# RMSNorm and matmul on one core: eight token tiles per transfer, gamma read first, two short reads halfway

## The chip, the core and the metric

The kernel runs on one core of a Trainium2 chip. Time is the device time of one execution in microseconds (us); the figure used is the median of ten runs. The profile is of one further execution.

A core has five engines that run side by side and wait for each other through semaphores. TensorE (PE) multiplies matrices, and its weight loads are shown as PEld. VectorE (DVE), ScalarE (ACT) and GpSimd (POOL) work on tiles. SyncE (SP) issues most of the transfers. The transfers between HBM and the core's memory run on 16 DMA engines, which every queue shares.

## What is computed

```python
# x: 16 x 1024 x 512 float32, gamma: 512 ones, weight: 512 x 768 float32, eps: 1e-5
rms = np.sqrt(np.mean(x ** 2, axis=-1, keepdims=True) + eps)
x_norm = x / rms * gamma
return np.matmul(x_norm, weight).astype(np.float32)
```

The output is 16 x 1024 x 768 float32. The kernel reads 33.6 MB of x and 1.6 MB of weights and writes 50.3 MB.

## The kernel before

**Tiling.** The 16,384 rows of x are 128 token tiles of 128 rows. A tile of x is 256 KB, a tile of the output 384 KB. The kernel works on pairs of tiles (`j`, 64 of them). Gamma is multiplied into the weights once (`weights`), so that a tile needs only its own row scale at the end.

**Work of one tile.** GpSimd casts x to bf16 (L85, a pair at a time). TensorE transposes the cast tile, taken as 32-bit words of two bf16 values (L112, two transposes a tile). VectorE copies the transposed words out of the accumulator memory (L119). ScalarE squares and sums the rows (L89) and takes the root (L93), VectorE the reciprocal (L95). TensorE then runs eight matmuls a tile, four of 512 and four of 256 columns (L146). The result is scaled by the reciprocal and written to an output tile: even tiles on ScalarE (L129), odd tiles on VectorE (L131). The transposes of later tiles are put between the matmuls (`feeder`).

**Transfers.** Consecutive tiles are grouped, `G = 4` to a group. `parts` says into how many transfers a group is cut: the first three and the last three groups are cut smaller, and all others are moved whole. In `rows` a transfer of t tiles gives each of the 128 partitions t rows that follow each other in HBM. A load of four tiles thus has 128 pieces of 8 KB, and a store of four tiles 128 pieces of 12 KB. Loads go into eight buffers of four tiles (`xin`), results into four buffers of four tiles (`out`). A group's store is issued when its last tile is scaled (L143).

**Order.** The order on each engine is written out by hand (`manual_schedule`); a loop iteration issues the load of the group four ahead, then the work of a pair. All loads and nearly all stores are issued by SP, in the order of the program, so a load that stands behind a store is issued after it. The last two tiles have four stores of their own, two on ScalarE's queue and two on SP's (L291). SP's and ScalarE's transfers take turns on eight completion semaphores: a transfer is issued only when the earlier one with the same semaphore has landed.

**Start.** The first tiles of x are loaded ahead of the weights, and gamma is read between them by ScalarE (L184). TensorE runs 14 matmuls on zeros (`warm_up`, L204) around the first transposes, and the transpose of gamma (L214) stands after the first three of them. The first three tiles are multiplied with the first half of the weights as soon as that is scaled.

Of the kernel before, what the change touches and what calls it, by code (L numbers as in the profile page):

```python
# [12 lines left out]
F32 = mybir.dt.float32  # L13
# [5 lines left out]
def kernel(  # L19
# [8 lines left out]
    nc = tc.nc  # L28
    P = 128

    x = x.flatten_outer_dims()
    out = out.flatten_outer_dims()
    N, D = x.shape
    _, O = out.shape
    K = D // P
    NT = N // P
    NP = NT // 2
    G = 4
    NG = NT // G
    PF = 5  # L40
    WIDE = 512

    parts = {0: [1, 2, 1], 1: [2, 2], 2: [2, 2], NG - 3: [2, 2], NG - 2: [2, 2], NG - 1: [1, 1, 1, 1]}
    first, size = {}, {}
    for g in range(NG):
        i = g * G
        for n in parts.get(g, [G]):
            for t in range(n):  # L50
# [3 lines left out]
    def rows(ap, i):  # L54
        return ap[first[i] * P:(first[i] + size[i]) * P, :].rearrange("(p t) d -> p t d", t=size[i])

    singles = ctx.enter_context(tc.tile_pool(name="singles", bufs=1))
    xin = ctx.enter_context(tc.tile_pool(name="xin", bufs=PF + 3))
    xbp = ctx.enter_context(tc.tile_pool(name="xb", bufs=4))
    junk = ctx.enter_context(tc.tile_pool(name="junk", bufs=2))  # L60
    stats = ctx.enter_context(tc.tile_pool(name="stats", bufs=4))
    xt_pool = ctx.enter_context(tc.tile_pool(name="xt", bufs=4))
    tpsum = ctx.enter_context(tc.tile_pool(name="tpsum", bufs=2, space=bass.MemoryType.PSUM))
    opsum = ctx.enter_context(tc.tile_pool(name="opsum", bufs=3, space=bass.MemoryType.PSUM))
    outp = ctx.enter_context(tc.tile_pool(name="out", bufs=4))

    x_tiles, xb_tiles, tp_tiles, rstd_of, xT_tiles, o_tiles = {}, {}, {}, {}, {}, {}

    def held(tiles, i, n=1):
        return tiles[i // G][:, i % G:i % G + n, :]  # L70

    def load(i):
        if i // G not in x_tiles:
            x_tiles[i // G] = xin.tile([P, G, D], F32, name="xt")
        nc.sync.dma_start(out=held(x_tiles, i, size[i]), in_=rows(x, i))

    def load_group(g):
        for i in range(g * G, (g + 1) * G):
            if first[i] == i:
                load(i)  # L80

    def cast(i, engine, n=1):
        if i // 2 not in xb_tiles:
            xb_tiles[i // 2] = xbp.tile([P, 2, D], BF16, name="xb")
        engine.tensor_copy(out=xb_tiles[i // 2][:, i % 2:i % 2 + n, :], in_=held(x_tiles, i, n))  # L85

    def square(i, ssq):
        jk = junk.tile([P, D], BF16, name="jk")
        nc.scalar.activation(out=jk, in_=held(x_tiles, i)[:, 0, :], func=AF.Square, accum_out=ssq)  # L89

    def root(i, n, ssq):
        rms = stats.tile([P, 4], F32, name="rms")
        nc.scalar.activation(out=rms[:, :n], in_=ssq[:, :n], func=AF.Sqrt, scale=1.0 / D, bias=eps_sb)  # L93
        rstd = stats.tile([P, 4], F32, name="rstd")
        nc.vector.reciprocal(out=rstd[:, :n], in_=rms[:, :n])  # L95
        for t in range(n):
            rstd_of[i + t] = rstd[:, t:t + 1]
# [24 lines left out]
    def transpose_tile(i):  # L122
        for h in range(2):
            transpose_word(i // 2, i % 2, h)
        evac(i // 2, i % 2, 1)

    def scale(engine, dst, src, r):
        if engine is nc.scalar:
            nc.scalar.mul(out=dst, in_=src, mul=r)  # L129
        else:  # L130
            nc.vector.tensor_single_scalar(out=dst, in_=src, scalar=r, op=mybir.AluOpType.mult)  # L131

    def accumulator():
        return opsum.tile([P, 2, WIDE], F32, name="ops").rearrange("p a b -> p (a b)")
# [15 lines left out]
    def matmuls(i, acc, ks, feed=None):  # L150
        for k in ks:
            matmul(i, k, acc, 0, WIDE)
            if feed:
                feed()
            matmul(i, k, acc, WIDE, O)
# [18 lines left out]
        return feed  # L174

    with tc.manual_schedule():

        wv = weight.rearrange("(h w c) o -> w h (c o)", w=P, c=2)
        touched = singles.tile([P, 2, 1], F32)
        nc.scalar.dma_start(out=touched, in_=wv[:, :, 0:1])  # L180
        load(0)
        load(1)
        g_row = singles.tile([2, P, 2], F32)
        nc.scalar.dma_start(out=g_row, in_=gamma.rearrange("(h w c) -> h w c", w=P, c=2))  # L184
        nc.scalar.preload_act_table(AF.Sqrt)  # L185
        w_f32 = singles.tile([P, K, O], F32)
        for h in range(2):
            nc.sync.dma_start(out=w_f32[:, 2 * h:2 * h + 2, :].rearrange("p c o -> p (c o)"), in_=wv[:, h, :])
        load(3)
        for g in range(1, PF):  # L190
            load_group(g)


        warm = singles.tile([P, WIDE], BF16)
        nc.vector.memset(warm, 0.0)  # L195
        eps_sb = singles.tile([P, 1], F32)
        nc.vector.memset(eps_sb, float(eps))  # L197
        ident_f = singles.tile([P, P], F32)
        make_identity(nc, ident_f)
        spare = accumulator()  # L200

        def warm_up(n):
            for _ in range(n):
                nc.tensor.matmul(out=spare[:, :WIDE], lhsT=warm[:, :P], rhs=warm, start=True, stop=True)  # L204

        w_bf = singles.tile([P, K, O], BF16)

        def weights(k, engine):
            scale(engine, w_bf[:, k, :], w_f32[:, k, :], g_sb[:, k % 2, k // 2:k // 2 + 1])

        warm_up(3)
        gp = tpsum.tile([P, 2, 2], F32, name="tp")
        for c in range(2):
            nc.tensor.transpose(out=gp[:, c, :], in_=g_row[:, :, c], identity=ident_f[:2, :2])  # L214
        g_sb = singles.tile([P, 2, 2], F32)
        nc.vector.tensor_copy(out=g_sb, in_=gp)  # L216
        warm_up(3)


        ssq = stats.tile([P, 4], F32, name="ssq")  # L220
        cast(0, nc.vector)
        square(0, ssq[:, 0:1])
        transpose_tile(0)
        warm_up(3)
        cast(1, nc.vector)
        cast(2, nc.gpsimd)
        square(1, ssq[:, 1:2])
        square(2, ssq[:, 2:3])
        transpose_tile(1)
        transpose_tile(2)  # L230
        warm_up(5)

        acc = [accumulator() for _ in range(4)]
        weights(0, nc.vector)
        weights(1, nc.scalar)
        for k in (0, 1):
            for i in range(3):
                matmuls(i, acc[i], [k])
        root(0, 3, ssq)
        weights(2, nc.vector)  # L240
        weights(3, nc.scalar)
        cast(3, nc.gpsimd)
        matmuls(0, acc[0], [2, 3])
        finish_tile(0, acc[0], nc.scalar)
        transpose_tile(3)
        norms(3, 1)
        matmuls(1, acc[1], [2, 3])
        finish_tile(1, acc[1], nc.vector)
        cast(4, nc.gpsimd)
        cast(5, nc.gpsimd)  # L250
        matmuls(2, acc[2], [2, 3])
        finish_tile(2, acc[2], nc.scalar)
        matmuls(3, acc[3], [0, 1, 2, 3], feeder([2], [0, 2, 2, 0], alone=True))
        finish_tile(3, acc[3], nc.vector)
        cast(6, nc.gpsimd, 2)
        cast(8, nc.gpsimd, 2)
        norms(4, 2)


        one, two, both = [1, 1, 0, 1, 1, 0, 0, 0], [1, 0, 1, 0, 1, 0, 1, 0], [1, 1, 1, 1, 1, 1, 1, 1]  # L260
        for j in range(2, NP):
            if j % 2 == 0 and j // 2 + PF - 1 < NG:
                load_group(j // 2 + PF - 1)
            if j + 3 < NP:
                cast(2 * j + 6, nc.gpsimd, 2)
            if j + 1 < NP:
                norms(2 * j + 2, 2)
            if j == NP - 1:
                break
            if j < 4:  # L270
                feed = feeder([j + 1], one)
            elif j == 4:
                feed = feeder([5, 6], both)
            elif j + 2 < NP:
                feed = feeder([j + 2], two)
            else:
                feed = None
            for i, engine in ((2 * j, nc.scalar), (2 * j + 1, nc.vector)):
                a = accumulator()
                matmuls(i, a, range(K), feed)  # L280
                finish_tile(i, a, engine)


        for i in (NT - 2, NT - 1):
            for lo, hi, engine, queue in ((0, WIDE, nc.scalar, nc.scalar), (WIDE, O, nc.vector, nc.sync)):
                a = accumulator()
                for k in range(K):
                    matmul(i, k, a, lo, hi)
                dst = out_tile(i)[:, lo:hi]
                scale(engine, dst, a[:, lo:hi], rstd_of[i])  # L290
                queue.dma_start(out=rows(out, i)[:, 0, lo:hi], in_=dst)  # L291
# [35 lines left out]
```

## Time and profile before

| what | value |
|---|---|
| median of 10 runs | 213.34 us (213.13 to 214.67) |
| the profiled execution's own time | 213.34 us |
| its span, first to last instruction | 211.6 us |
| TensorE busy | 200.6 us, 95% of the span |
| ScalarE busy | 158.1 us, 75% |
| VectorE busy | 111.3 us, 53% |
| GpSimd busy | 65.1 us, 31% |
| bytes moved | 85.70 MB, mean 405 GB/s |
| packets | 12,678 |

The span is what the page calls the time from the first to the last instruction. The run's own time is 1.7 us longer than that. The page divides the span into 40 slices of 5.3 us and gives the busy share of each engine in tenths for every slice, the mean busy share of the 16 DMA engines, and the rate at which they moved bytes. Another part of the page follows the chain of work that ended last back through the execution. Lists of groups give each kind of instruction with its count, its mean duration and what ended the idle time ahead of it.

### The profile page before, as it was taken

To read this page: it belongs to the slowest core of one execution; us is meant where nothing else is said; L and a number is where in the kernel's file an instruction comes from. 1 tells how busy PE (TensorE), PEld (TensorE's weight loads), DVE (VectorE), ACT (ScalarE), POOL (GpSimd) and SP (SyncE) were. 2 spreads that over 40 slices of the span, in tenths; PEclk is the share of its full clock that TensorE was granted. 3 is DMA by queue.
4 is the path that set the end of the run, shared out by engine and by line. 5 is a ranking of instruction groups with operands and counts; after the bars stand their busy time and mean duration, and the time that the engine had idled before them with its cause. 6 is when DMAs were issued, how large, how long until landed. Compare 5 with 4: busy or idle time off the path is not lost.

```text
span 211.6 us, 3631 instructions
## 1 busy us (share of the span) xinstructions
PE 200.6 (95%) x1271; PEld 138.5 (65%) x1296; DVE 111.3 (53%) x203; ACT 158.1 (75%) x388; POOL 65.1 (31%) x71
## 2 busy tenths in 40 slices
PE   5999999999999999999999999999999999999960
PEld 2566767766776677777667776776777777667630
DVE  1536556545654565456545654664466446545630
ACT  4469877877787778777877887788778877877830
POOL 2075332133332233333223333322233333223000
PEclk9999999999999999999999999999999999999996
DMA  6999999999999999999999999999999999999892
GB/s 233 410 419 369 419 421 423 395 429 412 428 424 420 422 417 428 424 426 421 430 428 417 420 426 425 428 424 424 431 422 429 428 423 419 417 420 414 342 385 112
DMA packets 12678, 85.70 MB, mean 405 GB/s; under 512 B 1650, under 2 KB 1908, under 8 KB 6004
## 3 DMA queue, kind: packets, MB, share of 16 engines
q1 hardware_dynamic: 12096, 84.94, 96.9%
q10 hardware_dynamic: 564, 0.53, 0.7%
q8 instruction: 10, 0.16, 0.3%
q14 instruction: 8, 0.07, 0.1%
HBM read 35.13 MB, written 50.33 MB: 404 GB/s over the span
## 4 chain that ended last, share of the span: by engine, by line
PE 93%; DMA 1%; DVE 1%; ACT 1%; issue 1%; ACTq 0%
PE ops L146 77%; PE tp L112 13%; PE ops L204 2%; DMA g_row<-in_gamma_dram 1%; DVE ot L131 1%; ACT ot L129 0%; ACT jk L89 0%; ACTq L180 0%; DVE xT L119 0%; PE tp L214 0%; ACT rms L93 0%; DVE rstd L95 0%
## 5 line engine op out<-in xcount | busy, mean ns | idle before, releaser
L146 PE MATMUL ops<-w_bf,xT 128*128 128x512 bf16 (+1 forms) x999 | 192.5, 324 | 1.3
L146 PEld LDWEIGHTS <-xT 128*128 128x128 bf16 x1024 | 100.3, 98 | 56.5 <-DVE xT L119 0.9
L85 POOL CAST xb<-xt 128x1024 bf16<-128x1024 f32 (+1 forms) x65 | 64.5, 1014 | 126.9 <-DMA xt<-in_x_dram 92.3
L119 DVE COPY xT<-tp 128x1024 bf16<-128x1024 bf16 (+1 forms) x67 | 44.6, 667 | 83.2 <-PE tp L112 83.1
L129 ACT ACTIVATE ot<-ops,rstd 128x768 f32<-128x768 f32 (+1 forms) x65 | 58.1, 894 | 38.9 <-PE ops L146 38.1
L89 ACT ACTIVATE jk<-xt 128x512 bf16<-128x512 f32 x128 | 78.8, 618 | 0.9 <-DMA xt<-in_x_dram 0.9
L112 PE MATMUL tp<-ident_f,xb 128*128 128x128 f32 x256 | 69.4, 276 | 0.1
L131 DVE TENSOR_SCALAR ot<-ops,rstd 128x768 f32<-128x768 f32 (+1 forms) x65 | 64.5, 992 | 2.9 <-PE ops L146 2.8
L112 PEld LDWEIGHTS tp<-ident_f,xb 128*128 128x128 f32 x256 | 36.4, 143 | 4.0 <-issue 0.7
L89 ACT ACTIVATION_READ_ACCUMULATOR jk<-xt 128x1 f32 x128 | 24.3, 190 | 0.0
L93 ACT ACTIVATE rms<-ssq,eps_sb 128x2 f32<-128x2 f32 (+1 forms) x64 | 18.9, 295 | 2.0
L95 DVE RECIPROCAL rstd<-rms 128x2 f32<-128x2 f32 (+1 forms) x64 | 9.9, 155 | 3.1 <-ACT rms L93 3.1
L204 PE MATMUL ops<-warm 128*128 128x512 bf16 x14 | 6.7, 624 | 1.2 <-DVE eps_sb L197 1.2
L129 ACT ACTIVATE w_bf<-w_f,g_sb 128x768 bf16<-128x768 f32 x2 | 1.9, 936 | 2.8 <-DVE xT L119 2.2
L204 PEld LDWEIGHTS <-warm 128*128 128x128 bf16 x14 | 1.8, 139 | 3.0 <-issue 1.7
L185 ACT ACT_TABLE_LOAD x1 | 1.3, 1283 | 1.9 <-issue 1.9
L216 DVE COPY g_sb<-tp 128x4 f32<-128x4 f32 x1 | 0.2, 163 | 3.1 <-PE tp L214 3.1
L214 PEld LDWEIGHTS tp<-ident_f,g_row 2*128 2x128 f32 x2 | 0.3, 201 | 2.1 <-issue 2.1
L214 PE MATMUL tp<-ident_f,g_row 2*128 2x2 f32 x2 | 0.4, 250 | 1.2 <-DMA g_row<-in_gamma_dram 1.2
L131 DVE TENSOR_SCALAR w_bf<-w_f,g_sb 128x768 bf16<-128x768 f32 x2 | 1.2, 614 | 0.5 <-DMA w_f<-in_weight_dram 0.5
L85 DVE CAST xb<-xt 128x512 bf16<-128x512 f32 x2 | 0.8, 416 | 0.0
L195 DVE MEMSET warm<- 128x256 uint32 x1 | 0.3, 272 | 0.9 <-PEq L308 0.9
(7 smaller groups left out, 1.0 us busy)
## 6 DMA issues: line engine op xcount, KB each, us to landing
out_dram<-ot SPq DMA_DIRECT2D x26, 1536.0 KB, 10.9
xt<-in_x_dram SPq DMA_DIRECT2D x26, 1024.0 KB, 12.7
out_dram<-ot SPq DMA_DIRECT2D x9, 768.0 KB, 9.3
xt<-in_x_dram SPq DMA_DIRECT2D x9, 512.0 KB, 10.5
xt<-in_x_dram SPq DMA_DIRECT2D x6, 256.0 KB, 12.5
w_f<-in_weight_dram SPq DMA_DIRECT2D x2, 768.0 KB, 7.3
out_dram<-ot SPq DMA_DIRECT2D x4, 384.0 KB, 7.7
out_dram<-ot ACTq DMA_DIRECT2D x2, 256.0 KB, 5.5
```

The source lines that it names most:

```text
L85: engine.tensor_copy(out=xb_tiles[i // 2][:, i % 2:i % 2 + n, :], in_=held(x_tiles, i, n))
L89: nc.scalar.activation(out=jk, in_=held(x_tiles, i)[:, 0, :], func=AF.Square, accum_out=ssq)
L93: nc.scalar.activation(out=rms[:, :n], in_=ssq[:, :n], func=AF.Sqrt, scale=1.0 / D, bias=eps_sb)
L95: nc.vector.reciprocal(out=rstd[:, :n], in_=rms[:, :n])
L112: nc.tensor.transpose(out=tp_tiles[j][:, t, h, :], in_=words[:, lo:lo + P], identity=ident_f)
L119: nc.vector.tensor_copy(out=dst[:, t:t + n, :], in_=src[:, t:t + n, :])
L129: nc.scalar.mul(out=dst, in_=src, mul=r)
L131: nc.vector.tensor_single_scalar(out=dst, in_=src, scalar=r, op=mybir.AluOpType.mult)
L146: nc.tensor.matmul(out=acc[:, lo:hi], lhsT=xT_tiles[i // 2][:, i % 2, k // 2, :, k % 2], rhs=w_bf[:, k, lo:hi], start=(k == 0), stop=(k == ...
L185: nc.scalar.preload_act_table(AF.Sqrt)
L204: nc.tensor.matmul(out=spare[:, :WIDE], lhsT=warm[:, :P], rhs=warm, start=True, stop=True)
L214: nc.tensor.transpose(out=gp[:, c, :], in_=g_row[:, :, c], identity=ident_f[:2, :2])
```

## The change

Groups become eight tiles instead of four. The first two groups and the last two are cut smaller. In the middle, from tile 16 to tile 111, each load and each store is one transfer of eight tiles, with 16 KB and 24 KB per partition. There are five input buffers of eight tiles and three output buffers of eight tiles. Loads are started by tile number (`load_until`) instead of by group. Gamma's read is the first on ScalarE's queue. Its transpose and copy move behind the transposes of tiles 0 to 2, the zero matmuls are arranged as 6, 3 and 6 instead of 3, 3, 3 and 5, and the scaling of the first quarter of the weights is cut in two. At pair 32 two reads of 5 and 6 rows of x go to a tile that nothing reads.

```diff
-    G = 4
+    G = 8
-    PF = 5
+    AHEAD = 20
-    parts = {0: [1, 2, 1], 1: [2, 2], 2: [2, 2], NG - 3: [2, 2], NG - 2: [2, 2], NG - 1: [1, 1, 1, 1]}
+    parts = {0: [1, 2, 1, 2, 2], 1: [4, 4], NG - 2: [4, 2, 2], NG - 1: [2, 2, 1, 1, 1, 1]}
...
-    xin = ctx.enter_context(tc.tile_pool(name="xin", bufs=PF + 3))
+    xin = ctx.enter_context(tc.tile_pool(name="xin", bufs=5))
-    outp = ctx.enter_context(tc.tile_pool(name="out", bufs=4))
+    outp = ctx.enter_context(tc.tile_pool(name="out", bufs=3))
...
+    starts = [i for i in range(NT) if first[i] == i]
+
+    def load_until(i):
+        while starts and starts[0] < i:
+            load(starts.pop(0))
...
+        g_row = singles.tile([2, P, 2], F32)
+        nc.scalar.dma_start(out=g_row, in_=gamma.rearrange("(h w c) -> h w c", w=P, c=2))
...
         nc.scalar.dma_start(out=touched, in_=wv[:, :, 0:1])
-        load(0)
-        load(1)
-        g_row = singles.tile([2, P, 2], F32)
-        nc.scalar.dma_start(out=g_row, in_=gamma.rearrange("(h w c) -> h w c", w=P, c=2))
...
+        load_until(3)
...
-        load(3)
-        for g in range(1, PF):
-            load_group(g)
+        load_until(AHEAD)
...
-        warm_up(3)
-        gp = tpsum.tile([P, 2, 2], F32, name="tp")
-        for c in range(2):
-            nc.tensor.transpose(out=gp[:, c, :], in_=g_row[:, :, c], identity=ident_f[:2, :2])
-        g_sb = singles.tile([P, 2, 2], F32)
-        nc.vector.tensor_copy(out=g_sb, in_=gp)
-        warm_up(3)
...
+        warm_up(6)
         cast(0, nc.vector)
...
-        warm_up(5)
+        gp = tpsum.tile([P, 2, 2], F32, name="tp")
+        for c in range(2):
+            nc.tensor.transpose(out=gp[:, c, :], in_=g_row[:, :, c], identity=ident_f[:2, :2])
+        g_sb = singles.tile([P, 2, 2], F32)
+        nc.vector.tensor_copy(out=g_sb, in_=gp)
+        warm_up(6)
...
-        weights(0, nc.vector)
+        weights(0, nc.vector, 0, WIDE)
+        weights(0, nc.vector, WIDE, O)
...
         for j in range(2, NP):
-            if j % 2 == 0 and j // 2 + PF - 1 < NG:
-                load_group(j // 2 + PF - 1)
+            load_until(2 * j + AHEAD)
+            if j == NP // 2:
+                marks = singles.tile([8, 2, 256], F32)
+                for c, n in enumerate((5, 6)):
+                    nc.sync.dma_start(out=marks[:n, c, :128 + 8 * c], in_=x[:n, :128 + 8 * c])
```

More of the change, by code (lines that the diff above doesn't have):

```diff
@@ L75, in load @@
         nc.sync.dma_start(out=held(x_tiles, i, size[i]), in_=rows(x, i))
[L77 to L80, printed above, removed]
+    starts = [i for i in range(NT) if first[i] == i]
+    def load_until(i):
+        while starts and starts[0] < i:
+            load(starts.pop(0))
     def cast(i, engine, n=1):
@@ L206, with weights @@
         w_bf = singles.tile([P, K, O], BF16)
-        def weights(k, engine):
-            scale(engine, w_bf[:, k, :], w_f32[:, k, :], g_sb[:, k % 2, k // 2:k // 2 + 1])
-        warm_up(3)
-        gp = tpsum.tile([P, 2, 2], F32, name="tp")
-        for c in range(2):
-            nc.tensor.transpose(out=gp[:, c, :], in_=g_row[:, :, c], identity=ident_f[:2, :2])
-        g_sb = singles.tile([P, 2, 2], F32)
-        nc.vector.tensor_copy(out=g_sb, in_=gp)
-        warm_up(3)
+        def weights(k, engine, lo=0, hi=O):
+            scale(engine, w_bf[:, k, lo:hi], w_f32[:, k, lo:hi], g_sb[:, k % 2, k // 2:k // 2 + 1])
         ssq = stats.tile([P, 4], F32, name="ssq")
+        warm_up(6)
         cast(0, nc.vector)
```

## The prediction

> **What bounds the kernel now.** I read the chain of waits first, then the DMA rows of the page, because TensorE cannot explain the end alone.
>
> ```profile
> PE 93%; DMA 1%; DVE 1%; ACT 1%; issue 1%; ACTq 0%
> DMA  6999999999999999999999999999999999999892
> q1 hardware_dynamic: 12096, 84.94, 96.9%
> ```
>
> The chain is TensorE for 93% of the span. But the DMA engines are in the top tenth of every slice from the second to the third from last, and SP's queue (q1) has 96.9% of 16 engines' span, about 205 us. Two things run without a gap. Which one ends last is read from the end, in the table by stretches of time and then in SP's own waits (engine and line, who it waited for, us in total, times, longest):
>
> ```profile
> core 0: us, PE busy (x) PEld busy (x) DVE busy (x) ACT busy (x) POOL busy (x), PEclk, DMA share, GB/s
> 160.00:180.00 20.00, 19.84 (x131) 13.97 (x133) 11.17 (x21) 15.65 (x40) 7.78 (x8) 1.00 1.01 424
> 200.00:205.00 5.00, 4.43 (x28) 2.48 (x26) 2.51 (x5) 2.47 (x4) 0.00 (x0) 1.00 0.88 358
> 205.00:211.60 6.60, 0.00 (x0) 0.00 (x0) 0.00 (x0) 0.00 (x0) 0.00 (x0) 0.73 0.43 162
> ...
> SPq L291 <- DMA out_dram<-ot: 5.0, 1, 5.0
> ```
>
> TensorE's last matmul ends near 204.4 us; after 205 there is only DMA, 6.6 us of it. SP issues its last store only after waiting 5.0 us for another store. The DMA rows of 203 to 212 us, in 40 parts, show how that drain ends:
>
> ```profile
> DMA  9899999999999999983122111111103930000000
> GB/s 437 355 410 396 410 410 410 355 423 391 373 396 405 355 328 432 364 332 114 68 82 82 73 59 50 46 50 50 50 32 137 355 100 0 0 0 0 0 0 0
> ```
>
> The engines are full to about 207, then the rate falls to 50 GB/s for 2 to 3 us: one or two of sixteen engines are behind, and every transfer's landing waits for the slowest. The landing marks in the trace say the same. ScalarE's first tail store, issued at 203.45, has half its marks by 206.58 and its last at 208.97; SP issues the store that waits for it at 209.04, it lands at 210.73, and the span ends 0.83 later. Stores issued at 36.5 and 182.5 took 10.4 and 12.8 us, so the backlog grows. **The end is a DMA backlog that lags TensorE**, on the slowest engines; TensorE's own end is only 7.2 us ahead of it.
>
> **The change part by part.** The sum is made against the profiled execution, 213.34 us with a span of 211.56; its own time equals the median.
>
> *Fewer, larger transfers.* SP issues 84 transfers now and 60 afterwards, two of which are the short reads: loads fall from 41 to 28 and stores from 39 to 26 beside the two tail stores and two of weights. Bytes stay the same. I sorted the trace's single packets by size (medians on one engine): 2 KB 84 ns, 4 KB 159, 8 KB 309, 12 KB 460. That is a line: (460 - 309) / 4096 = 0.0369 ns per byte, or 27.1 GB/s and 434 on sixteen engines, plus 309 - 302 = 7 ns a packet. Each transfer also has one mark per engine, 9 ns. A transfer of 128 rows has 8 packets on each engine, so one transfer fewer saves 8 x 7 + 9 = 65 ns of every engine, and 26 fewer save **1.69 us**. Nothing hides that: the queue is not empty from 2 us on, so an engine that needs 1.69 us less ends 1.69 us sooner, unless the larger packets cost more. No packet of 16 or 24 KB on SP's queue is in the trace. If they are cut up inside, the saving is 0. If they run on the same line, it is 1.69. I take 1.69, since four sizes lie on the line; a loss is the rival below.
>
> Two rules of the Trainium skill were weighed here, both of "DMA: Bandwidth & Descriptors". Section "Measured" has 341 GB/s for 1 MB and 425 for 16 MB, with a fixed 2 us per transfer. By that rule 26 fewer would be worth up to 52 us. The row is 424 GB/s with transfers of 1 and 1.5 MB queued behind each other: the fixed part is already overlapped, and the row decides. The rule against the change is in "Latency and other measured facts"[...]. Loads go from 8 to 16 KB between partitions and stores from 12 to 24, far below; and here the 8 KB packets (a power of two) lie on the line of the 12 KB ones. Price by the trace: nothing.
>
> *Later stores, earlier loads.* A load is now issued right behind the store of tiles that end 25 before its first one. At the issue of a store, eight more tiles of loads are queued or done than before: 2.1 MB, 4.9 us at 425 GB/s. Stores then land up to 12.8 + 4.9 = 17.7 us after issue. An output buffer is written again 16 tiles after its store; at 6.07 us for four tiles (SP's issues) that is 24.3 us: margin 6.6. A load behind it lands within 17.7 + 4.9 = 22.6 us and its first cast is needed about 19 tiles after the issue, 28.8 us: margin 6. In the start, tiles 16 to 23 now arrive together: 16 to 19 land at 22.46 now, 1.05 MB more make it 24.9, and TensorE turns to their transposes near 30. Tiles 8 to 11 land together at 15.8 and tile 8 is transposed near 21. So TensorE waits for none of these; price 0. If that cover went, a late load would stop TensorE for the lateness.
>
> Is the DMA ever idle for want of stores? At the end of tile 111 (182.45) the loads are all issued in both kernels, so the same bytes remain, and 16 tiles of stores, 6.3 MB or 14.8 us, still follow the 12.8 us of backlog. Price 0.
>
> *Gamma first, zero matmuls 6, 3, 6.* Now TensorE idles from 2.65 to 3.88 for gamma, and VectorE's cast of tile 0 stands behind gamma's copy (4.28), though x has landed at 3.4. Afterwards the cast starts near 3.4. Cold zero matmuls come every 0.427 us, and they fill TensorE from 7.1 to 9.7, so the first real matmul moves from 10.08 to about 9.7. If TensorE's pace doubles sooner (0.427 to 0.216 us for 512 columns near 10 us now), the bound is the weights: landed 8.20, first cut scaled by 8.7, a start 1.4 us earlier. One more VectorE instruction costs below 0.1 us. Either way TensorE ends 0.4 to 1.4 us earlier while the backlog ends last: worth 0 to the end.
>
> *Short reads.* 11 rows of about half a KB, some 30 ns each on at most six engines, and two SP issues of 0.4 us with no wait open before them. At most 0.06 us; 0 taken.
>
> *The tail's semaphores.* In the instruction order the last SP store waits for ScalarE's first tail store. Afterwards the turn falls one earlier, and both last SP stores wait for it. They then go out one after the other: an issue of 0.33 and a gap of 0.1 add **0.4 us** behind that landing.
>
> Sum: 208.97 - 1.69 = 207.28 landing; issues at 207.35 and 207.8; 1.69 to land: 209.5; end 210.3 against 211.56. The time becomes 213.34 - 1.3 = **212.0 us**.
>
> **Rivals.**
>
> *The lag stays.* Only one or two engines set the end. What they lost came in single packets (one of 1.33 us at 4.7, two near 1.2 us at 18.6 and 43.8), which may fall otherwise. Against it: ten runs within 0.2% but for one. If the slowest engine gets 1.3 us worse in relation to the others, nothing is left: 213.2, no change.
>
> *Larger rows move slower.* Slower side: one mechanism, in the middle, 96 of 128 tiles, 62.9 MB. If 16 and 24 KB rows ran at 414 GB/s, twice the 207 that the skill's row gives for its mildest pitch, the middle would take 62.9 / 0.414 - 62.9 / 0.425 = 3.9 us more: about 216. It decides from 1.3 us on, when packets are 1% off the line. For it: 8 KB packets near 17 to 19 us took up to 0.6 us. Against: 90% of them stay within 4% of the line.
>
> *The shared semaphore alone.* If packets save nothing and the turn costs 0.4: 213.8.
>
> *TensorE sooner and the slow engines less behind.* ScalarE's tail store cannot land much before 206.4 (its first mark), 0.9 less than I take, or 1.5 if TensorE ends early: 210.7.
>
> **How the numbers follow.** A difference under 0.2% (0.43 us) cannot be told from no change. Forecast, 211.2 to 212.8: 0.56. Lag stays, 213.2: 0.18. Larger rows slower, 214 to 217: 0.10. Semaphore alone: 0.06. Sooner, 210.4 to 211.2: 0.10. The range 210.5 to 213.7 leaves out the slower rows and little else. Faster 0.65 (forecast and the last), same 0.19, slower 0.16.
>
> **What would show it.** Right: near 8,400 packets on q1 with a share lower by 1.7 us of 16 engines, rate above 425 GB/s in the middle, 16 KB packets near 611 ns and 24 KB near 913, TensorE without new idle time, the first real matmul at 9.7 or sooner, SP's last wait at a landing near 207.3. Wrong: packet times off the line, POOL or ScalarE stopping TensorE for a late load or an output buffer, or the same last landing with fewer packets.

## The result and the profile after

| | before | after |
|---|---|---|
| median of the runs compared | 213.31 us (213.06 to 214.67, 32 runs) | 212.28 us (212.13 to 212.57, 9 runs) |
| ratio to before, with its 95% interval | | 0.9952 (0.9941 to 0.9962) |
| profiled execution, and its span | 213.34, 211.6 | 212.74, 211.0 |

The change gains 1.03 us, 0.5%. The profiled execution of after lies 0.46 us above the median of its runs, so the two traces differ by 0.6 us where the medians differ by 1.03. The same kernel was profiled again later ("after_again", below): 212.46 us, span 210.6.

The page of after, the same rows as were shown of before (chain by engine, busy tenths of the DMA engines in 40 slices, and SP's queue with packets, MB and share of 16 engines):

```profile
DMA  6999999999999999999999999999999999999891
...
q1 hardware_dynamic: 8374, 84.94, 96.3%
...
PE 92%; DMA 1%; DVE 1%; ACT 1%; issue 1%
```

3,722 packets fewer carry the same 84.94 MB. 96.9% of 211.56 us was 205.0 us; 96.3% of 210.96 is 203.2. The engines are nearly as full as before and need less time. The table by stretches of time:

```profile
core 0: us, PE busy (x) PEld busy (x) DVE busy (x) ACT busy (x) POOL busy (x), PEclk, DMA share, GB/s
160.00:180.00 20.00, 19.89 (x132) 14.08 (x133) 10.85 (x20) 16.28 (x40) 6.24 (x6) 1.00 1.00 413
200.00:205.00 5.00, 3.09 (x20) 1.67 (x17) 1.98 (x3) 1.51 (x3) 0.00 (x0) 1.00 1.00 401
205.00:211.00 6.00, 0.00 (x0) 0.00 (x0) 0.00 (x0) 0.00 (x0) 0.00 (x0) 0.79 0.23 85
```

TensorE now ends at 203.1, 1.3 us sooner, and is busy 3.09 of the 5 us from 200 (4.43 before). After 205 the DMA share is 0.23 where it was 0.43: much of the time after the last matmul is now spent with empty engines. SP's waits (who it waited for, us in total, times, longest) and the DMA rows of 203 to 212 us in 40 parts show where:

```profile
SPq L291 <- DMA out_dram<-ot: 6.0, 1, 6.0
SPq L75 <- POOL xb L86: 2.1, 3, 1.3
```

```profile
DMA  9999999998421111111000000295960000000000
GB/s 396 410 437 364 351 401 364 419 387 355 164 82 50 50 50 50 64 41 46 27 27 9 0 0 0 86 346 182 350 201 0 0 0 0 0 0 0 0 0 0
```

```profile
207.93 0.81 SPq L291 DMA_DIRECT2D out_dram<-ot  x2
```

The rate falls from full at 205.3 to 50 GB/s, as before; that is the slowest engines' drain. It reaches 0 at about 208. Then there is a hole of some 0.7 us, and a second bump: SP's last two stores (the timeline line: start, us, two issues), which had to wait until ScalarE's first tail store landed at 207.87. (Tail stores are the four stores of the last two tiles. Drain is the time in which the engines work off what was issued before.) Before, the last drain ran on under the one store that waited. Now the drain is over first.

The landing marks put numbers on it: each of the 16 engines leaves one, and a store has landed with the last. Landings are the last marks, for the two profiled executions:

| store | before | after |
|---|---|---|
| tile 125 (SP) | 209.55 | 207.67 |
| tile 126, first part (ScalarE's first) | 208.97 | 207.87 |
| tile 127, first part (ScalarE's second) | 210.15 | 208.30 |
| SP's first of its two, issued at | 203.68 | 207.93 |
| SP's last, issued at | 209.04 | 208.36 |
| SP's last, landed | 210.73 | 210.12 |
| end of the span | 211.56 | 210.96 |

Most engines are not late in either trace. Half the marks of tile 125's store are there 2.78 us after its issue before, and 2.74 after the change; the last comes 6.64 and 6.09 us after the issue. What is left of the backlog at the end sits on a few engines.

### The profile page after: what moved, and what is told of

Its sections match the earlier page's. It is cut to its first block, busy times and chain, and to the rows that moved or that the text cites. A ratio compares the mean times of both kernels' runs of the same rounds, so it can differ in the third digit from the quotient of the medians.

```text
span 211.0 us, 3584 instructions
## 1 busy us (share of the span) xinstructions
PE 200.1 (95%) x1272; PEld 138.2 (66%) x1297; DVE 111.7 (53%) x204; ACT 158.2 (75%) x388; POOL 66.1 (31%) x71
## 3 DMA queue, kind: packets, MB, share of 16 engines
q1 hardware_dynamic: 8374, 84.94, 96.3%
## 4 chain that ended last, share of the span: by engine, by line
PE 92%; DMA 1%; DVE 1%; ACT 1%; issue 1%
PE ops L147 77%; PE tp L113 13%; DMA xt<-in_x_dram 1%; PE ops L202 1%; DVE ot L132 1%; ACT ot L130 0%; DVE xT L120 0%; ACT jk L90 0%; DVE xb L86 0%; PE tp L224 0%; ACT rms L94 0%; DVE rstd L96 0%
## 5 line engine op out<-in xcount | busy, mean ns | idle before, releaser
L86 POOL CAST xb<-xt 128x1024 bf16<-128x1024 f32 (+1 forms) x65 | 65.4, 1014 | 120.7 <-PE tp L113 61.9
L202 PE MATMUL ops<-warm 128*128 128x512 bf16 x15 | 5.7, 531 | 1.2 <-DVE eps_sb L195 1.2
L132 DVE TENSOR_SCALAR w_bf<-w_f,g_sb 128x512 bf16<-128x512 f32 (+2 forms) x3 | 1.4, 484 | 0.0
## 6 DMA issues: line engine op xcount, KB each, us to landing
out_dram<-ot SPq DMA_DIRECT2D x12, 3072.0 KB, 15.5
xt<-in_x_dram SPq DMA_DIRECT2D x12, 2048.0 KB, 19.8
```

## The experiments

Each kernel was timed beside the kernel before on its own chip; ratios are to that, with 95% intervals. There were three batches, and before measured 213.32, 213.36 and 213.27 in them.

**The start and the large transfers, each alone.** head_only is the kernel before with the changed start (the diff, against before); large_only is the changed kernel with the old start (the reverse, against after).

```diff
+        g_row = singles.tile([2, P, 2], F32)
+        nc.scalar.dma_start(out=g_row, in_=gamma.rearrange("(h w c) -> h w c", w=P, c=2))
...
-        warm_up(3)
-        gp = tpsum.tile([P, 2, 2], F32, name="tp")
...
-        warm_up(3)
+        warm_up(6)
...
         transpose_tile(2)
-        warm_up(5)
+        gp = tpsum.tile([P, 2, 2], F32, name="tp")
...
+        warm_up(6)
...
-        weights(0, nc.vector)
+        weights(0, nc.vector, 0, WIDE)
+        weights(0, nc.vector, WIDE, O)
```

> The kernel before with the new start alone (gamma first, its transpose behind tiles 0 to 2, zero matmuls 6, 3, 6, first weights in two cuts). Drain theory (the end is the DMA backlog of the slowest engine, and what the change saves is 65 ns per transfer left out): TensorE starts its real matmuls near 8.7 us and ends near 203.1, the time stays within 0.4 us of before, 212.9 to 213.4. Start theory (the gain is TensorE's earlier start): 212.0 to 212.4, all of the gain.

> The changed kernel with the old start: large transfers, buffers, load order and short reads alone. Drain theory: 212.1 to 212.6, all of the gain, with TensorE starting at 10.1 and ending near 204.4. Start theory: 213.3 or, with the later semaphore, 213.7.

Measured: head_only 213.36 us, ratio 0.9999 (0.9989 to 1.0008), 22 runs. large_only 212.61, 0.9962 (0.9952 to 0.9972), 22 runs. The start alone is worth nothing that can be measured, although it works: the first real matmul of head_only begins at 8.28 (10.08 before), and ScalarE's first tail store is issued at 201.75 (203.45 before). In large_only the old start was itself sooner than expected (first real matmul at 9.31, TensorE's end at 203.66), and its time is 0.01 us above the range that was expected. The DMA rows of head_only, 203 to 212, and SP's wait for a store at the tail:

```profile
DMA  9999999999543233221100000881000000000000
GB/s 423 382 364 401 364 423 360 405 369 414 205 159 150 109 118 146 105 77 50 59 32 23 32 23 23 287 301 37 23 23 23 5 0 0 0 0 0 0 0 0
```

```profile
SPq L291 <- DMA out_dram<-ot: 5.4, 1, 5.4
```

From the bump of the last store (near 208.9) to about 210 a rate of 23 GB/s remains, less than one engine's 27 on the line of the prediction: one engine is still at work on stores issued long before. Tile 125's store landed at 209.79, SP's first tail store at 210.12, the last at 210.43. ScalarE's store was issued 1.7 us sooner, and the last mark came 0.3 us sooner (210.73 before). So TensorE's end was not the bound of the kernel before, the drain was, and the gain belongs to the large transfers, all of it or nearly all. large_only and the full change (0.9962 and 0.9952) have overlapping intervals; the traces show no gain from the start either, since ScalarE's first tail store landed at 207.52 in large_only though it was issued at 202.68, 0.6 us later than in after.

**The size of a transfer, the rest unchanged.** pieces4 moves the middle as transfers of four tiles, pieces2 as transfers of two, in the changed kernel with its buffers of eight. The diff is that of pieces4; pieces2 has [2, 2, 2, 2] there.

```diff
-        for n in parts.get(g, [G]):
+        for n in parts.get(g, [4, 4]):
```

> The changed kernel with each group of eight in the middle moved as two transfers of four (8 and 12 KB per partition again), everything else as changed. 24 transfers more. Drain theory: 24 x 65 ns = 1.56 us more, less 0.43 because the turn of the semaphores falls as before: 213.4. Start theory, or a gain from buffers and load order: 212.3.

> The changed kernel with each group of eight in the middle moved as four transfers of two tiles (4 and 6 KB per partition). 72 transfers more than the changed kernel, 48 more than with pieces of four. Theory (65 ns per transfer on every engine, drain sets the end): 48 x 65 ns = 3.1 us over the pieces of four (213.24): 216.0 to 216.6. Rival (a step between sizes, not a price per packet): 213.2 to 214, or with eight semaphores for more transfers a stall that takes it over 218.

| transfers in the middle | kernel | median us | ratio | mean time of an engine's data packets, one trace |
|---|---|---|---|---|
| 24 | after | 212.28 | 0.9952 (0.9941 to 0.9962) | 203.95 |
| 48 | pieces4 | 213.24 (22 runs) | 0.9994 (0.9984 to 1.0004) | 204.43 |
| 96 | pieces2 | 215.67 (4 runs) | 1.0105 (1.009 to 1.012) | 207.24 |

With transfers of four tiles the gain is gone, with its new buffers, its new start and its short reads still in place. From 48 to 96 transfers the time rises by 2.43 us, 51 ns a transfer (the sum in the prediction: 65 on every engine); pieces2 came out 0.33 us below the range that was expected of it. From 24 to 48 it rises by 0.96, or 0.78 against after_again, where 24 x 65 ns less the 0.43 us of the semaphore turn, which pieces4 does not have, would be 1.13.

The DMA rows of pieces4, 203 to 212, show where the time went:

```profile
DMA  9999999999896220000000000049200000000000
GB/s 410 382 382 423 369 401 369 373 341 410 346 419 246 82 91 18 23 23 36 23 23 23 23 32 23 23 177 355 91 27 23 23 0 0 0 0 0 0 0 0
```

From 206.4 to 210 us the rate is about that of a single engine, but for the bump of the last store. The packets of the two traces leave the same bytes at 200 us, 2.54 MB in pieces4 and 2.53 in after. The difference is how late the slowest engine is: it lands tile 125's store at 209.96 in pieces4, and at 207.06 to 209.24 in the five traces with transfers of eight and the same tail. pieces2 on the page, and SP's waits:

```profile
q1 hardware_dynamic: 18742, 84.95, 96.9%
```

```profile
SPq L144 <- DMA out_dram<-ot: 32.2, 22, 1.7
SPq L75 <- DMA xt<-in_x_dram: 19.3, 25, 0.9
```

SP here waits dozens of times for the completion of its own earlier transfers, which with 24 transfers it does not. The queue still stays full (96.9% of a span of 213.6), and the packets alone need 2.81 us more of each engine than in pieces4. So it is the packets that make it slower, not these waits.

**The tail's wait.** These variants put all four tail stores on one queue, to take SP's wait for ScalarE's store away. The diff, all four on SP, is that of tail_sp and tail_sp_again (made to after), before_tail_sp (to before) and large_tail_sp (to large_only). tail_act puts all four on ScalarE's queue, with nc.scalar at the end of both.

```diff
-            for lo, hi, engine, queue in ((0, WIDE, nc.scalar, nc.scalar), (WIDE, O, nc.vector, nc.sync)):
+            for lo, hi, engine, queue in ((0, WIDE, nc.scalar, nc.sync), (WIDE, O, nc.vector, nc.sync)):
```

> The changed kernel with all four tail stores issued by ScalarE, so that none waits for another's landing. Drain theory with the semaphore wait as its last link: the last store goes out near 203.7 and lands with the slowest engine near 208.5 instead of 210.1; time 210.6 to 211.0. Rival (the last stores would be as late on any queue, because the slowest engine is): 212.0 to 212.4.

> The changed kernel with all four tail stores issued by SP. Each then shares its semaphore with a store that landed long before, and none waits. Theory (after the change the slowest engine has drained by 208.3 us and the rest up to 210.1 is the wait for ScalarE's store): last landing near 208.5 to 209.0, time 210.7 to 211.2. Rival (the slowest engine is as late without the wait): 212.1 to 212.4.

> The kernel before with the same edit: all four tail stores issued by SP, no wait between them. Theory (there the slowest engine itself is busy until 210.3 us, so the wait costs next to nothing): 213.0 to 213.3, at most 0.3 less. Rival (the wait is what sets the end in both kernels): about 211.8.

tail_act measured 212.29 us (211.54 to 214.49, 22 runs), 0.995 (0.9933 to 0.9968): no gain over after, which refutes the expectation. SP's waits and the DMA rows of 203 to 212 show why:

```profile
SPq L144 <- DMA out_dram<-ot: 6.6, 1, 6.6
```

```profile
DMA  9999513999961100059999989920000000000000
GB/s 391 419 351 346 196 46 118 405 364 369 341 232 50 41 27 18 23 209 410 396 410 423 382 355 423 410 82 0 0 0 0 0 0 0 0 0 0 0 0 0
```

The wait did not go away; it moved to earlier stores. Now the stores of tiles 124 and 125 (L144, in the ordinary loop) have their turn of the semaphores behind two of ScalarE's. They go out at 206.09 and 206.52, behind landings at 206.03 and 206.38, and run alone until 209.4. The rate shows two dips in place of one hole.

tail_sp measured 212.01 (211.39 to 214.45, 22 runs), 0.9938 (0.9921 to 0.9955). Its profiled execution (211.61) has its last landing at 208.99, as expected, but the median was expected at least 0.8 us lower. before_tail_sp, the same edit in the kernel before, measured 213.35 (22 runs), 1.001 (0.9995 to 1.0025): there the wait cost nothing. Because the runs of tail_sp spread more than after's, it was run once more beside after, and on the old start too:

> The changed kernel once more, on the same chip and beside the three others of this call, so that their differences can be read. 212.1 to 212.5 by every theory.

> The changed kernel with the four tail stores on SP once more, on the same chip as the changed kernel. Theory (the wait costs what the slowest engine leaves of it, which differs from run to run): 0.2 to 0.5 us below the changed kernel, with a wider spread. Rival (no difference, the first was chance): within 0.1 us of it.

> Large transfers with the old start, and the four tail stores on SP. Theory (the earlier start gained 0.3 us only because the semaphore chain begins with TensorE's end; without the chain the drain sets the end and the start is worth nothing): the same as with the new start, 211.8 to 212.2. Rival (the start is worth 0.3 us by itself): 0.3 us above the changed kernel with its tail on SP.

| kernel, one chip | median us | ratio |
|---|---|---|
| after_again | 212.46 (212.18 to 212.74, 7 runs) | 0.9958 (0.9943 to 0.9973) |
| tail_sp_again | 211.73 (211.51 to 212.51, 6 runs) | 0.9927 (0.9906 to 0.9948) |
| large_tail_sp | 211.44 (211.37 to 212.62, 6 runs) | 0.9919 (0.9897 to 0.9941) |

tail_sp_again, SP's timeline at the end and the DMA rows of 203 to 212:

```profile
199.25 2.73 SPq L144 DMA_DIRECT2D out_dram<-ot  x3
202.18 2.55 SPq L291 DMA_DIRECT2D out_dram<-ot  x4
```

```profile
DMA  9999999999989931121111000000000000000000
GB/s 369 396 423 382 355 437 382 337 369 387 423 341 337 337 118 64 73 77 73 55 46 55 32 23 23 0 0 0 0 0 0 0 0 0 0 0 0 0 0 0
```

All four stores are out by 204.7, there is one drain without a hole, and the last mark is at 209.07 (209.82 in after_again). So the wait that cost nothing before costs something after the change: 0.73 us side by side on one chip, 0.27 (tail_sp against after) and 1.17 (large_tail_sp against large_only) across chips. The last two runs gained more than was expected of them. The intervals of tail_sp_again and after_again still overlap (0.9943 to 0.9948); those of large_tail_sp and large_only, each beside before on its own chip, do not (0.9897 to 0.9941, and 0.9952 to 0.9972). That the wait costs time after the change rests on the three pairs together, and its size is uncertain. Which of the two starts is better with the tail on SP these runs cannot tell.

**The short reads.**

```diff
-            if j == NP // 2:
-                marks = singles.tile([8, 2, 256], F32)
-                for c, n in enumerate((5, 6)):
-                    nc.sync.dma_start(out=marks[:n, c, :128 + 8 * c], in_=x[:n, :128 + 8 * c])
```

> The changed kernel without the two short reads of 5 and 6 rows. Theory (they cost some 0.06 us of six engines and the turn of the semaphores at the tail is the same): 212.1 to 212.4. Rival (they shift the semaphores or the engines' shares to good effect): 212.7 or more.

> The changed kernel without the two short reads, beside the changed kernel. Theory (the short reads do nothing for the time, and the 212.63 of six runs was the spread between chips): within 0.15 us of the changed kernel. Rival (the short reads gain some 0.3 us): 212.5 to 212.8 with the changed kernel at 212.3.

no_marks measured 212.63 (6 runs), 0.9967 (0.9954 to 0.998), on the second chip, between the two ranges that were expected; so it was repeated. no_marks_again measured 212.45 (6 runs), 0.9955 (0.9939 to 0.9972), beside 212.46 of after_again on the third. The reads do nothing that can be measured. A row of them takes 27 to 29 ns on an engine.

## Why the prediction was right

It said 212.0 us and the median is 212.28, inside the likeliest case. By its steps:

- **The bound.** A DMA backlog on the slowest engines, not TensorE: shown by head_only (ScalarE's tail stores 1.7 us earlier, no gain) and by pieces4 (only the transfer size put back, gain gone).
- **65 ns per transfer.** The typical packets lie on the line: 16 KB takes 611 ns (611 predicted) and 24 KB 912 (913), both medians. The data packets of an engine needed 205.64 us before and 203.95 after, which looks like the 1.69 that was predicted. That is luck of the pair: this sum leaves out the marks, so the line gives 1.46 for it, and head_only and before_tail_sp, with the same transfers as before, need 204.75 and 204.91. With the marks, an engine needs 205.35 to 206.56 us in the four traces with transfers of four, and 203.95 to 205.15 in the nine with transfers of eight. The middles lie 1.23 apart.
- **The term that was mis-sized** is most likely these 65 ns. They come from medians, but a sum of packets follows the mean. The mean 16 KB packet took 625 ns in the middle one of the nine traces and the mean 24 KB packet 921, 14 and 9 above their medians; 8 and 12 KB lie only 6 and 3 above (315 and 463, middle of four traces). By these means one large packet in place of two saves about 5 ns, and a transfer 8 x 5 + 9, an estimate of 50 ns in place of 65: 1.3 us for 26 of them. From pieces4 to pieces2 the time grew by 51 ns a transfer, though an engine's packets and marks grew by 68. With the tail on one queue in both kernels, and so no wait, before_tail_sp and tail_sp are 1.34 us apart on one chip; but tail_sp_again and large_tail_sp, on another chip, lie 1.62 and 1.91 below before_tail_sp. So the size is between 1.3 and 1.9 by these pairs, and the runs do not settle it. That the slowest engine saves less than the mean one is possible too, but the traces do not name the engines.
- **The landing of ScalarE's first tail store.** The prediction has 208.97 - 1.69 = 207.28. In the five executions profiled with this tail and the large transfers (after, after_again, large_only and the two without short reads) it came at 207.87, 207.47, 207.52, 207.52 and 207.30. The middle one is 1.45 earlier than before. That is not the saving of the transfers alone, since this store was also issued 0.8 to 1.6 us sooner: in head_only, issued 1.7 sooner and with the old transfers, it landed at 207.74, while the slowest engine went on until 210.4.
- **The rival of slower large rows** did not come true as a price, since the kernel is faster and the medians are on the line. It has a part in the difference of 15 ns: SP's queue has 28 to 47 packets of over 1 us with transfers of eight, and at most 3 with smaller ones. In after, 20 of its 31 lie between 20 and 40 us and between 160 and 180, and there its rate is 409 and 413 GB/s (423 and 424 before). Between 40 and 160 us it is 425 to 431 (415 to 427 before). The prediction put this term at nothing because 8 KB packets lie on the line of the 12 KB ones, which was too little to go by. The row of the Trainium skill that it weighed ("DMA: Bandwidth & Descriptors", "Latency and other measured facts") does not speak of such rows: it has 207 GB/s per direction at a distance of 512 KiB, against 214 in full with padded rows, and 103, half, only at 4 and 8 MiB. No run here has rows so far apart.
- **The 2 us per transfer** that the prediction weighed and set aside would have made up to 52 us of 26 transfers; about 1 came. The same page has that figure in "Anatomy of one DMA — SWDGE (gpsimd) path", not in "Measured", and both sections are on transfers issued by GpSimd. Here SP and ScalarE issue them.
- **The semaphore turn, +0.4.** In after both last SP stores were issued behind the landing of ScalarE's first tail store, 0.43 apart (207.93, 208.36). From ScalarE's landing to the last landing it took 2.25 us; the prediction's sum has 2.22.
- **The sum.** The middle one of the five last landings (209.56, 209.77, 209.78, 209.82, 210.12) is 209.78 where 209.5 was predicted. That is 0.28 us, and so is the difference between 212.28 and 212.0; that they agree so well is chance, since these five executions have a middle time of 212.46. (The chances of the forecast and of "sooner" add to 0.66, not to 0.65.)
- **The start, 0.** First real matmul at 8.74 and TensorE's end 1.34 us sooner, inside the 0.4 to 1.4 given; worth nothing alone (head_only), and nothing that could be told apart in the changed kernel (large_only against after, large_tail_sp against tail_sp_again).
- **Later stores, earlier loads, 0.** Stores of eight tiles took 15.5 us and loads 19.8 (medians; the longest that can be read are 15.5 and 19.9), below the 17.7 and 22.6 that were allowed, and TensorE has no new idle time. One wait was not foreseen: three loads waited for GpSimd's cast to free an input buffer, 2.1 us in all (the line of L75 above). In after_again it was 0.2 us, and that kernel was not faster for it.
- **The short reads, 0.** Confirmed side by side in no_marks_again.

What the sum held without saying it: by making the drain shorter and the turn longer, the change moves the bound of the last 2 us from the slowest engine to the chain of issue, landing and issue. In four of the five executions all stores but SP's last two had landed 1.4 to 1.8 us before the end of the last; in after_again one engine was at work on tile 125's store until 209.24, 0.6 before it. That is why a fix of the tail gains after the change (0.3 to 1.2 us in three pairs) and nothing before it.

Open is why one or two of the sixteen engines fall 2 to 6 us behind by the end. Single packets of over 1 us were seen (0.3 to 0.9 us is usual), but not what causes them. Ten packets of 16 KB on the queue that the page calls "instruction" (q8) took 0.88 to 1.12 us each before, 9.9 us in all, enough to put a few engines behind if they fell on these. The traces do not say which engine carries a packet, and no run here separated them. It decides how much of a saving on every engine arrives at the end.

## What to carry to other kernels

When transfers are queued without a gap, their count has a price even in a hidden stage: sort the packets of the trace by size and fit a line. What is left per packet and per transfer, times the count, is the gain to expect. Take the means as well as the medians: here they give 50 and 65 ns a transfer, and 51 arrived from pieces4 to pieces2. A new wait at the tail took 0.4 us of the gain. After shortening a backlog look at the tail again for waits that it covered, in the DMA rate: a hole before the last bump is a wait that may now cost time. An earlier start was worth nothing here, where the end is set by a queue that is full from the beginning.

## What was not expected of the hardware

- **TensorE's pace at the start.** It doubles (zero matmuls from 0.427 to 0.216 us) at moments that differ between executions: with the same start order the first real matmul began at 10.08 (before), 9.14 (before_tail_sp), 9.31 (large_only) and 9.40 (large_tail_sp). In after it had doubled when the last six zero matmuls ran:

```profile
7.44 1.47 PE L202 MATMUL ops<-warm 128*128 128x512 bf16 x6
8.74 1.03 PE L147 MATMUL ops<-w_bf,xT 128*128 128x512 bf16 x5
```

  So the prediction's 9.7 was the bound for the pace not having doubled. What came is set by the six zero matmuls at the doubled pace, 0.216 us apart, the last from 8.53 to 8.74. The weights, which the prediction names as the other bound, were ready before: landed at 7.02 instead of 8.20, their first cut scaled by 8.23. In before a packet of theirs took 1.33 us.
- **The turn of the completion semaphores is not that of the program when a second queue takes part.** In tail_act the stores of tiles 124 and 125 stand earlier in the program than the four tail stores, and yet they waited for two of these. Moving stores to another queue can so move a wait to an earlier store.
